# Row maxima of attention scores: small transfers in place of diagonal blocks, products with ones and row copies

## The chip, the cores and the metric

One core of a Trainium2 chip runs the kernel in one launch. The metric is the device time of one launch in microseconds (us); lower is better. The engines are PE (TensorE: matrix products), DVE (VectorE), ACT (ScalarE), POOL (GpSimd) and SP, which here only issues transfers (DMAs). Each engine works through its own list of instructions in order; semaphores hold an instruction back until what it needs is there.

## The reference

Two layers of a decoder trunk, 528 tokens (16 learned meta tokens and 512 real ones), width 1024. Each layer is a mixer (attention with 8 heads of 64, a 31-tap convolution group, a short gated convolution group, all from one input projection) and a gated feed-forward part with a 3-tap convolution. What matters here is the attention:

```python
F = jnp.cumsum(log_f, axis=1).transpose(0, 2, 1)
def attend(start, end):
    qb = q[:, start:end]
    s = jnp.einsum("bqhd,bkhd->bhqk", qb, k[:, :end]) * scale
    s = s + F[:, :, start:end, None] - F[:, :, None, :end]
    s = jnp.where(mask, s, NEG_INF)
    p = jax.nn.softmax(s, axis=-1)
    return jnp.einsum("bhqk,bkhd->bqhd", p, v[:, :end])
outs = [attend(0, N_META)]
for i in range((L - N_META) // Q_BLOCK):     # four blocks of 128 queries
    ...
```

The softmax needs for each query the maximum of its row of scores, so that the exponentials stay in range.

## The kernel before

Activations lie transposed: features on the 128 partitions, 528 tokens along the free dimension. Float32 accuracy comes from splitting each operand into a high and a low part, so that one product of the mathematics is three matrix products (`mm3`, L837; the value projection has its own loop, L1407). Most of the run is such products of a 128x128 block of weights with 264 tokens.

Each head has two query tiles and two key tiles (`qh[hd % 4]`, `kh[hd % 4]`, 128 partitions x 528). Half of the first pair's partitions hold the head's 64 features (high parts); some of the other partitions hold extra rows, among them the forget-gate sums on the key side. One extra row, `mrow` (`rows(hd)[2]`), is all ones in the key tile and, in the query tile, first zero and later minus the maximum of the query's row of scores. So the product of the two tiles gives scores less their maximum without a further instruction.

The mixer's work is written as threads: Python generators that yield what they wait for. A planner (`Flow`) steps them by a cost per instruction and thereby fixes the order of the instructions on each engine; on the chip this order is fixed and only the semaphores decide the times. Four threads matter. `maxima` and `exponentials` go head by head; `att_norms` normalises finished pairs of heads; `fill` makes the projections (blocks of 48 products, and 120 for the values) and so keeps PE at work while attention waits.

`maxima` before, for one head: five blocks of queries (`QB`: 16, then four of 128). For each block PE multiplies queries with keys (L1593; the last block takes two products), DVE takes the maximum of each row, with the causal mask added, into a column of `mcol` (L1600), one query to a partition. The maxima then have to come from a column into a row. POOL multiplies the identity with the column and with -1 into a block of the diagonal tile `dm` (L1608); PE multiplies `dm` with a matrix of ones, in two halves of 264 tokens, so that every row of the result holds all 528 negative maxima (L1617); ACT copies one row of it into `mrow` of the query tile (L1619). `maxima` of a head starts when `exponentials` of the head before has begun.

`exponentials` for one head: six blocks; per block PE makes the scores in two products (`logits`, L1637, the first reads `mrow`), ACT takes the exponential (L1644), POOL clears what lies above the diagonal (L1651), and two blocks later PE multiplies with the values (`weigh`, L1671; the trace records two instructions for each).

Transfers on SP in the mixer: weight blocks (`raw<-in_w_dram`, L785), gate rows (`k<-sq` and `k<-g_dram`, L699, from `gate_rows`), and for heads 2 to 7 the split projections of a pair of heads, from `pair_hi` and `pair_lo` into the query and key tiles (`part` and `spread`, L1499). The planner costs a gate row at `ROW_US` = 0.95 us of SP and the pair transfers at `PART_US` = 0.6 us and 2.2 us to landing. The query and key products of head 2 wait for the first `k<-pair_hi` of its pair. PSUM has two banks (`s1`) that `maxima`, the products with ones and the attention norms share.

Of the kernel before, what the change touches and what calls it, by code (L numbers as in the profile page):

```python
# [10 lines left out]
F32 = mybir.dt.float32  # L11
F32R = mybir.dt.float32r
BF16 = mybir.dt.bfloat16
AF = mybir.ActivationFunctionType
ALU = mybir.AluOpType

P = 128
D = 1024
KD = D // P
L = 528  # L20
N_META = 16
H = L // 2
# [40 lines left out]
PART_US, ROW_US = 0.6, 0.95  # L63
# [293 lines left out]
def mm_us(n, k=P):  # L357

    return max(n / 2400 + 0.012, 0.00086 * k)
# [7 lines left out]
def act_us(n):  # L367
    return 0.17 + 0.0009 * n
# [21 lines left out]
def tile_hybrid_trunk(ctx: ExitStack, tc: tile.TileContext, xT, wflat, pv_d, out):  # L390
    nc = tc.nc
# [3 lines left out]
    def T(pool, shape, dt, tag, bufs=None):  # L395
        uid[0] += 1
        kw = {} if bufs is None else {"bufs": bufs}
        return pool.tile(list(shape), dt, tag=tag, name=f"{tag}_{uid[0]}", **kw)
# [46 lines left out]
    ident = T(const, [P, P], F32, "ident")  # L445
    make_identity(nc, ident)
    def mset(t, val):
        nc.gpsimd.memset(t.bitcast(F32), val)
# [33 lines left out]
    flow = Flow()  # L482
# [5 lines left out]
    def half_sl(hf):  # L488
        return slice(H * hf, H * (hf + 1))
# [199 lines left out]
    def act(us, fn, *after, **kw):  # L689
        return flow.op("act", us, fn, after, **kw)  # L690
# [4 lines left out]
    def gp(us, fn, *after, **kw):  # L695
        return flow.op("pool", us, fn, after, **kw)
# [428 lines left out]
    def mixer(l, ypool, first, close_first, spans, front, rzs, u_at):  # L1125
# [125 lines left out]
        def bank(kind):  # L1251

            slot = yield from flow.grab(banks[kind])
            return psum[:, slot.buf], slot
# [104 lines left out]
        def rows(hd):  # L1359

            main = DH * (hd % 2)
            aux = DH - main
            return slice(main, main + DH), slice(aux, aux + DH), slice(aux + 32, aux + 33)

        for i in range(4):
# [3 lines left out]
            mset(kh[i][0][mrow], 1.0)  # L1369
            mset(qh[i][0][aux:aux + 32], 1.0)  # L1370
            mset(qh[i][0][aux + 32:aux + 64], 0.0)
        dms = []
        for j in range(2):
            dm = T(ap, [P, L], F32R, f"dm{j}")
            mset(dm[:, :N_META], 0.0)
            dms.append(dm)
        g_hl = [T(mp, [P, L], F32, "sq", 2)[:HEADS].bitcast(F32R) for _ in range(2)]

        v_at = {}
# [196 lines left out]

        def maxima():

            dm_at = {}
            for hd in range(HEADS):  # L1580
                yield [When(lambda: k_at.get(hd)), When(lambda: q_at[hd] if hd // 2 in k2_at else None),
                       When(lambda: gate_at.get(hd))] + ([When(lambda: begun.get(hd - 1))] if hd else [])
                q1, k1 = qh[hd % 4][0], kh[hd % 4][0]
                dm = dms[hd % 2]
                mcol = T(mp, [P, 6], F32, "mcol", 2)
                diag = []
                for b, (qs, n) in enumerate(QB):
                    end = qs + n
                    pieces = [(0, end)] if end <= 512 else [(0, H), (H, end)]
                    for i, (a, z) in enumerate(pieces):  # L1590
                        s, slot = yield from bank("s1")
                        s = s[:n, :z - a]
                        nc.tensor.matmul(s, lhsT=q1[:, qs:end], rhs=k1[:, a:z], start=True, stop=True)  # L1593
                        tok = flow.mm(mm_us(z - a, n))
                        last = z == end

                        def reduce(s=s, n=n, a=a, z=z, last=last, i=i, b=b):
                            junk = T(mp, [P, 400], BF16, "junk")
                            c0 = 400 - P + n - (z - a) if last else 0
                            nc.vector.tensor_tensor_reduce(  # L1600
                                junk[:n, :z - a], in0=s, in1=causal[:n, c0:c0 + z - a], scale=1.0,
                                scalar=-3e38 if i == 0 else mcol[:n, 5:6], op0=ALU.add, op1=ALU.max,
                                accum_out=mcol[:n, b:b + 1] if last else mcol[:n, 5:6])

                        d = dve(dve_us(z - a) + 0.08, reduce, tok, prio=0)
                        slot.close(d)
                        yield
                    diag.append(gp(0.5, lambda qs=qs, end=end, n=n, b=b: nc.gpsimd.tensor_scalar(  # L1608
                        dm[:n, qs:end], in0=ident[:n, :n], scalar1=mcol[:n, b:b + 1],
                        scalar2=-1.0, op0=ALU.mult, op1=ALU.mult), d, *dm_at.get(hd - 2, [zero])))  # L1610
                yield diag
                mrow = rows(hd)[2]
                toks, at = [], []
                for hf in range(2):
                    ps, slot = yield from bank("s1")
                    c = half_sl(hf)
                    nc.tensor.matmul(ps[:, :H], lhsT=ones_r, rhs=dm[:, c], start=True, stop=True)  # L1617
                    toks.append(flow.mm(mm_us(H)))
                    at.append(act(act_us(H), lambda ps=ps, c=c: nc.scalar.copy(q1[mrow, c], ps[mrow, :H]), toks[-1], prio=0))  # L1619
                    slot.close(at[-1])  # L1620
                    yield
                dm_at[hd] = toks
                max_at[hd] = at

        begun = {}
# [865 lines left out]
```

## Time and profile before

| | us |
|---|---|
| median of 3 runs (lowest, highest) | 1263.05 (1262.51, 1263.3) |
| span of the profiled execution, first to last instruction | 1262.4 |
| PE busy | 1243.7 (99%) |
| DVE, ACT, POOL busy | 926.1, 710.3, 174.6 |
| maxima and exponentials of layer 0 lie at about | 79 to 210 |
| and of layer 1 at about | 706 to 840 |

The profile gives no total for its execution beside the span; the span is 0.65 us under the median of the runs, and what is told of the span is applied to the median. Matrix products are pipelined, so that a busy PE can still lose time between products: a product of 264 tokens is recorded as about 0.28 us long, while the next one starts 0.12 us after it. The chain of work that ended last counts such products at their spacing.

### The profile page before, as it was taken

How to read it: one execution, taken by the hardware profiler on the slowest of the kernel's cores; microseconds unless marked ns; L12 is line 12 of the kernel's file. 1: busy time of each engine (PE TensorE's matmuls, PEld its weight loads, DVE VectorE, ACT ScalarE, POOL GpSimd, SP SyncE). 2: the span in 40 equal slices, each digit the busy share in tenths (PEclk: the TensorE clock that was granted, in tenths of full speed). 3: DMA queues.
4: the chain of work that ended last, by engine and by line, in shares of the span. 5: the costliest groups of instructions: out<-in, count | busy, mean ns of one | idle time of the engine just before them, and what ended most of it. 6: DMA issues, size and time to landing. Idle time of an engine off the chain costs nothing.

```text
span 1262.4 us, 24292 instructions
## 1 busy us (share of the span) xinstructions
PE 1243.7 (99%) x9554; PEld 1194.0 (95%) x9554; DVE 926.1 (73%) x1581; ACT 710.3 (56%) x1377; POOL 174.6 (14%) x360
## 2 busy tenths in 40 slices
PE   8999999999999999999999999999999999999997
PEld 8998898999999999999999988999999899989997
DVE  7887866589874776487688878656799748756964
ACT  7254576655444663476673545775554447526763
POOL 1323411001111001010003244120021000000000
PEclk9999999999999999999999999999999999999999
DMA  7357551726648755776652584547166565465611
GB/s 245 82 155 173 126 119 44 259 87 149 186 147 334 244 193 149 240 195 169 208 189 67 156 194 110 144 111 241 71 163 176 146 218 170 153 223 182 203 60 67
DMA packets 80755, 206.59 MB, mean 164 GB/s; under 512 B 8624, under 2 KB 18992, under 8 KB 80128
## 3 DMA queue, kind: packets, MB, share of 16 engines
q1 hardware_dynamic: 66976, 168.20, 42.1%
q0 software_dynamic: 13664, 36.84, 13.0%
q8 instruction: 75, 1.23, 0.4%
q14 instruction: 40, 0.33, 0.1%
HBM read 170.82 MB, written 50.60 MB: 175 GB/s over the span
## 4 chain that ended last, share of the span: by engine, by line
PE 89%; DVE 3%; issue 3%; DMA 2%; ACT 2%; POOL 1%; SPq 0%; DVEq 0%; POOLq 0%; ACTq 0%
PE psum L837 58%; PE psum L2288 17%; PE psum L1407 5%; PE psum L1671 3%; PE psum L1637 2%; PE psum L974 1%; PE psum L1593 1%; DMA raw<-in_w_dram 1%; PE psum L1737 1%; PE psum L1323 1%; DMA w_split<-slo 0%; DMA h<-in_w_dram 0%; POOL dm L1608 0%; DVE yp L1050 0%; DMA h<-in_x_dram 0%
## 5 line engine op out<-in xcount | busy, mean ns | idle before, releaser
L837 PE MATMUL psum<-y,whi 128*128 128x264 f32 (+3 forms) x1968 | 383.8, 299 | 0.8 <-DVE zs L989 0.7
L837 PEld LDWEIGHTS psum<-y,whi 128*128 128x128 f32 x1968 | 305.6, 188 | 13.8 <-DVE zs L989 0.9
L837 PE MATMUL psum<-uhi,whi 128*128 128x264 f32 (+1 forms) x1168 | 292.1, 289 | 1.5 <-ACT uhi L2069 0.7
L837 PE MATMUL psum<-ulo,whi 128*128 128x264 f32 (+1 forms) x1168 | 285.7, 284 | 0.6 <-DVE ulo L2071 0.4
L837 PE MATMUL psum<-uhi,wlo 128*128 128x264 f32 (+1 forms) x1168 | 285.1, 283 | 0.0
L837 PE MATMUL psum<-y,wlo 128*128 128x264 f32 (+3 forms) x984 | 273.7, 297 | 0.3 <-DVE wlo L793 0.3
L837 PEld LDWEIGHTS psum<-uhi,whi 128*128 128x128 f32 x1168 | 201.5, 188 | 6.2 <-issue 1.6
L837 PEld LDWEIGHTS psum<-ulo,whi 128*128 128x128 f32 x1168 | 201.6, 188 | 1.3 <-DVE ulo L2071 0.6
L837 PEld LDWEIGHTS psum<-uhi,wlo 128*128 128x128 f32 x1168 | 201.3, 188 | 0.0
L837 PEld LDWEIGHTS psum<-y,wlo 128*128 128x128 f32 x984 | 177.8, 188 | 5.8 <-DVE wlo L793 0.6
L2173 DVE SCALAR_TENSOR_TENSOR c<-zs,pv,c 128x528 f32<-128x528 f32 (+1 forms) x176 | 130.6, 756 | 23.5 <-ACT c L2171 22.2
L652 ACT CAST whi<-raw 128x1024 fp32r<-128x1024 f32 (+1 forms) x65 | 66.1, 1020 | 97.1 <-PE psum L837 74.5
L793 DVE TENSOR_TENSOR wlo<-raw,whi 128x1024 fp32r<-128x1024 f32 (+2 forms) x80 | 95.6, 1203 | 29.7 <-ACT whi L789 29.2
L789 ACT CAST whi<-raw 128x1024 fp32r<-128x1024 f32 (+2 forms) x80 | 81.7, 1031 | 24.9 <-PE psum L837 18.0
L653 DVE TENSOR_TENSOR wlo<-raw,whi 128x1024 fp32r<-128x1024 f32 (+1 forms) x65 | 76.9, 1183 | 21.1 <-ACT whi L652 21.0
L1153 DVE SCALAR_TENSOR_TENSOR cacc<-apad,pv,cacc 128x528 f32<-128x528 f32 x120 | 87.6, 772 | 0.1
L2288 PE MATMUL psum<-uhi,whi 128*128 128x258 f32 (+1 forms) x252 | 71.3, 284 | 0.0
L2288 PE MATMUL psum<-ulo,whi 128*128 128x258 f32 (+1 forms) x252 | 71.2, 283 | 0.0
L2288 PE MATMUL psum<-uhi,wlo 128*128 128x258 f32 (+1 forms) x252 | 70.7, 283 | 0.0
L2171 ACT ACTIVATE c<-zs,pv 128x528 f32<-128x528 f32 (+1 forms) x88 | 63.0, 727 | 6.8 <-DVE zs L2136 2.7
L2206 POOL COPY cols<-y 128x1 f32<-128x1 f32 x24 | 17.2, 716 | 335.8 <-ACT y L2187 335.5
L2288 PE MATMUL psum<-t,shi 128*128 128x258 f32 (+1 forms) x336 | 63.2, 283 | 0.0
(273 smaller groups left out, 2323.9 us busy)
## 6 DMA issues: line engine op xcount, KB each, us to landing
raw<-in_w_dram SPq DMA_DIRECT2D x114, 512.0 KB, 4.5
raw<-in_w_dram SPq DMA_DIRECT2D x30, 448.0 KB, 5.1
h<-in_w_dram SPq DMA_DIRECT2D x25, 512.0 KB, 4.5
raw<-w_sum SPq DMA_DIRECT2D x21, 512.0 KB, 5.4
h<-w_sum SPq DMA_DIRECT2D x21, 512.0 KB, 4.8
h<-in_w_dram POOLq DMA_DIRECT2D x16, 512.0 KB, 4.6
w_sum<-h POOLq DMA_DIRECT2D x16, 512.0 KB, 6.4
w_sum<-in_w_dram SPq DMA_DIRECT2D x26, 256.0 KB, 5.2
```

Source lines behind the costliest of these rows:

```text
L652: nc.scalar.copy(hi[:, :sz], raw[:, :sz])
L653: last_low[0] = nc.vector.tensor_sub(lo[:, :sz], raw[:, :sz], hi[:, :sz].bitcast(F32))
L789: nc.scalar.copy(box["hi"][:, :sz], box["raw"][:, :sz])
L793: nc.vector.tensor_sub(lo[:, :sz], box["raw"][:, :sz], box["hi"][:, :sz].bitcast(F32))
L837: nc.tensor.matmul(d, lhsT=w[a][:, k, cols], rhs=rhs(b, k, hf), start=start and i == 0 and p == 0, stop=stop and i == n - 1 and p == 2)
L1153: nc.vector.scalar_tensor_tensor(conv[j], in0=src, in1=conv[j], scalar=col("a_dw_w", CK * j + i), op0=ALU.mult, op1=ALU.add)
L1407: nc.tensor.matmul(ps[:n, :nw], lhsT=(uhi, ulo)[ui][:, k, P * b:P * b + n], rhs=w[wi][:, k % 4, :], start=k == 0 and p == 0, stop=k == KD ...
L1637: nc.tensor.matmul(s, lhsT=k[:, ka:ka + kn], rhs=q[:, s0:qz], start=i == 0, stop=i == 1)
L1671: nc.tensor.matmul(acc[:, s0 - qa:qz - qa], lhsT=vals[:, b].rearrange("p h d -> p (h d)")[:, o:o + P], rhs=box["p"], start=b == 0, stop=b ...
L2171: nc.scalar.activation(dst, src[:, 2:2 + 2 * fw], AF.Copy, scale=wtap(2, t))
L2173: nc.vector.scalar_tensor_tensor(dst, in0=src[:, i:i + 2 * fw], scalar=wtap(i, t), in1=dst, op0=ALU.mult, op1=ALU.add)
L2288: nc.tensor.matmul(psum[:, bank, :n7], lhsT=w[a][:, k0 + k, :], rhs=rhs(b, k), start=start and k == 0 and p == 0, stop=stop and k == K2 - ...
```

## The change

For each head, the diagonal blocks, the two products with ones and the two row copies go. In their place POOL negates the columns of maxima into a small tile `neg` in three instructions (after blocks 0, 2 and 4), and SP issues five transfers, one for each block of queries, that bring a column of `neg` (one element on each of up to 128 partitions) into the block's part of the row `mrow` of the query tile (up to 128 elements on one partition). The planner costs each at 0.95 us of SP and 3.5 us to landing, and makes a new order with them. The two tiles `dm` and their memsets go too. `neg` is doubled between heads as `mcol` is.

```diff
-        dms = []
-        for j in range(2):
-            dm = T(ap, [P, L], F32R, f"dm{j}")
-            mset(dm[:, :N_META], 0.0)
-            dms.append(dm)
...
-                dm = dms[hd % 2]
                 mcol = T(mp, [P, 6], F32, "mcol", 2)
-                diag = []
+                neg = T(mp, [P, 5], F32R, "neg", 2)
+                at = []
                 for b, (qs, n) in enumerate(QB):
...
-                    diag.append(gp(0.5, lambda qs=qs, end=end, n=n, b=b: nc.gpsimd.tensor_scalar(
-                        dm[:n, qs:end], in0=ident[:n, :n], scalar1=mcol[:n, b:b + 1],
-                        scalar2=-1.0, op0=ALU.mult, op1=ALU.mult), d, *dm_at.get(hd - 2, [zero])))
-                yield diag
-                mrow = rows(hd)[2]
-                toks, at = [], []
-                for hf in range(2):
-                    ps, slot = yield from bank("s1")
-                    c = half_sl(hf)
-                    nc.tensor.matmul(ps[:, :H], lhsT=ones_r, rhs=dm[:, c], start=True, stop=True)
-                    toks.append(flow.mm(mm_us(H)))
-                    at.append(act(act_us(H), lambda ps=ps, c=c: nc.scalar.copy(q1[mrow, c], ps[mrow, :H]), toks[-1], prio=0))
-                    slot.close(at[-1])
-                    yield
-                dm_at[hd] = toks
+                    if b in (0, 2, 4):
+                        mrow = rows(hd)[2]
+                        b0 = max(b - 1, 0)
+                        c = gp(0.2, lambda n=n, b0=b0, b=b: nc.gpsimd.tensor_scalar(
+                            neg[:n, b0:b + 1], in0=mcol[:n, b0:b + 1], scalar1=-1.0, scalar2=None, op0=ALU.mult), d)
+                        for i in range(b0, b + 1):
+                            qa, m = QB[i]
+                            at.append(flow.op("sp", ROW_US, lambda i=i, qa=qa, m=m: nc.sync.dma_start(
+                                q1[mrow, qa:qa + m].bitcast(F32), neg[:m, i:i + 1].bitcast(F32)), (c,), lat=3.5))
                 max_at[hd] = at
```

The new order is another one all through both mixers. Two places carry the prediction. The first is SP at the start of layer 0's attention. Before, the gate rows of heads 1 to 3 (`k_84`, `k_86`, `k_88`) are followed by two weight blocks and the copies for a sum of weights:

```order
L699 DMA k_84_698<-sq_733 1x16x33
L699 DMA k_86_700<-sq_732 1x16x33
L699 DMA k_86_700<-sq_733 1x16x33
L699 DMA k_88_702<-sq_732 1x16x33
L699 DMA k_88_702<-sq_733 1x16x33
L785 DMA raw_1155<-in_w_dram 128x1024
L785 DMA raw_1180<-in_w_dram 128x1024
L545 DMA w_sum_12_104_736<-in_w_dram 128x512 x2
```

Now the same stretch of SP holds head 0's five transfers (`q_90`) among the gate rows, and head 1's five (`q_92`) behind the copies (the changed kernel's L1609 is the new transfer):

```order
L1609 DMA q_90_704<-neg_1074 1x16x1
L699 DMA k_88_702<-sq_728 1x16x33
L1609 DMA q_90_704<-neg_1074 1x128x1 x2
L699 DMA k_88_702<-sq_729 1x16x33
L1609 DMA q_90_704<-neg_1074 1x128x1 x2
L785 DMA raw_1203<-in_w_dram 128x1024
L785 DMA raw_1217<-in_w_dram 128x1024
L545 DMA w_sum_12_102_732<-in_w_dram 128x512 x2
L545 DMA w_sum_12_102_732<-in_w_dram 128x1024
L1609 DMA q_92_706<-neg_1228 1x16x1
L1609 DMA q_92_706<-neg_1228 1x128x1 x4
```

The two weight blocks now stand behind head 0's last transfer, which waits for head 0's last maxima.

The second place is PE ahead of head 2's maxima (key tile `k_86`, query tile `q_94`). Before, PE is in the block of weights `whi_1147`, the one after the keys' block of this pair of heads, and 30 of its products stand between the last product of the keys' block and the first row of L1593 below:

```order
L837 MATMUL psum_67<-uhi_108,whi_1147 128x264
L837 MATMUL psum_67<-ulo_109,whi_1147 128x264
L837 MATMUL psum_67<-uhi_108,wlo_1162 128x264
L1593 MATMUL psum_67<-k_86_700,q_94_708 16x16
L1593 MATMUL psum_67<-k_86_700,q_94_708 128x144
```

Now the last product of the keys' block (`whi_1058`) is followed by nine rows of head 1's exponentials (L1625 is the scores, L1659 the product with the values, in the changed kernel's numbers), and then by head 2's maxima (L1587):

```order
L837 MATMUL psum_67<-uhi_108,wlo_1080 128x264
L1625 MATMUL psum_67<-q_92_706,k_84_698 128x128
L1625 MATMUL psum_67<-q_93_707,k_85_699 128x128
L1659 MATMUL psum_67<-p_79_687,vals_681 128x16
L1625 MATMUL psum_67<-q_92_706,k_84_698 128x400
L1625 MATMUL psum_67<-q_93_707,k_85_699 128x400
L1659 MATMUL psum_67<-pf_1381,vals_681 128x128
L1625 MATMUL psum_67<-q_92_706,k_84_698 128x400
L1625 MATMUL psum_67<-q_93_707,k_85_699 128x400
L1659 MATMUL psum_67<-pf_1392,vals_681 128x400
L1587 MATMUL psum_67<-k_86_700,q_94_708 16x16
L1587 MATMUL psum_67<-k_86_700,q_94_708 128x144
```

The 30 products moved behind head 2's first maxima. Layer 1 has the same two places in the same order.

More of the change, by code (lines that the diff above doesn't have):

```diff
@@ L1577, in maxima @@
         def maxima():
-            dm_at = {}
             for hd in range(HEADS):
```

## Prediction

> **What bounds the kernel now.** I read the busy shares first, then the two mixers in windows, then the instructions that go, then PE's waits, then the chain at the places that the new order changes. The page's first part and the two windows of the mixers (busy us of each engine with their counts, granted clock, DMA share, GB/s):
>
> ```profile
> PE 1243.7 (99%) x9554; PEld 1194.0 (95%) x9554; DVE 926.1 (73%) x1581; ACT 710.3 (56%) x1377; POOL 174.6 (14%) x360
> 76.80:213.50 136.70, 134.34 (x984) 122.32 (x984) 101.26 (x247) 85.86 (x224) 42.06 (x92) 1.00 0.50 124
> 706.00:840.50 134.50, 131.66 (x965) 120.14 (x964) 101.38 (x245) 83.55 (x220) 45.47 (x95) 1.00 0.58 139
> ```
>
> PE is the bound, in the mixers too: it is idle for 2.4 us of 136.7 and 2.8 us of 134.5, at full clock. ACT, DVE and POOL have a quarter of the time or more to spare, and the transfers take half of the DMA engines. So what leaves ACT and POOL is worth nothing by itself; what leaves PE counts, and so does each wait that comes or goes on PE.
>
> The instructions that go (count, then min/median/max in ns, first and last start), and PE's largest waits:
>
> ```profile
> L1608 POOL TENSOR_SCALAR dm<-ident,mcol x80: 267/372/1980, 80.9 to 819.8; 128x128 fp32r<-128x128 f32 x64, 16x16 fp32r<-16x16 f32 x16
> L1617 PE MATMUL psum<-dm,ones_r x32: 279/288/485, 84.3 to 829.9; 128*128 128x264 f32 x32
> L1619 ACT CAST q<-psum x32: 364/370/374, 84.8 to 830.2; 1x264 fp32r<-1x264 f32 x32
> PE psum L1617 <- POOL dm L1608: 1.4, 2, 1.0
> PE psum L1593 <- issue: 1.2, 1, 1.2
> PE psum L1593 <- DMA k<-pair_hi: 1.1, 1, 1.1
> PE psum L1323 <- ACT q L1619: 0.8, 2, 0.4
> ```
>
> Two of these four waits belong to what goes: PE waits for the diagonal, and a norm's product (L1323) waits for the bank that the row copy still holds. The other two are one wait, seen in each layer: head 2's maxima wait for the keys of their pair.
>
> **The change part by part.** *Products with ones.* In the chain, products are told at their spacing:
>
> ```profile
> 84.18 0.45 PE psum L1323 x2
> 84.63 0.25 PE psum L1617 x2
> 101.42 7.62 PE psum L837 x63
> ```
>
> Two products with ones take 0.25 us, the same 0.12 each as L837 (7.62/63 = 0.121). The record of 0.288 us is the length in the pipe, not the price. 32 of them are 32 x 0.121 = 3.9 us of PE. Gain: 3.9 us. A bound from above is 32 x 0.288 = 9.2, but that counts overlapped time, so I leave it out of the range.
>
> *Waits that go.* 1.4 us (diagonal) and 0.8 us (row copy), both PE's own. Gain: 2.2 us; from below nothing, if the same bank or DVE holds PE up elsewhere.
>
> *ACT, POOL, DVE.* ACT loses 32 x 0.37 = 11.8 us, POOL 80 diagonal blocks, and gets 48 small negations. Nothing shows one of this shape; the nearest rows are a memset of 128x16 (below) and the diagonal block's 0.372. I take 0.3 us, near the second, since both read and write a column; the range of 0.12 to 0.37 matters only in the latency below. DVE's list keeps its 96 maxima. All of this is beside PE: 0 us. The cover is PE's products, and if it were gone POOL's part would be worth what the waits above show.
>
> *SP.* 80 more issues, on a queue that is mostly idle, held by its buffers (258.2 us in the row below for one pair of lines alone). Rows: the memset; the gate rows' issues in layer 1 (one row of 528 numbers each) and their landing; the landing of all pair transfers; SP's longest wait.
>
> ```profile
> L448 POOL MEMSET dm<- x4: 116/117/118, 57.4 to 688.1; 128x16 f32 x4
> L699 SPq DMA_DIRECT2D k<-sq x8: 497/542/585, 702.3 to 708.9; - x8
> DMA to landing us min/median/max: 2.0/2.0/2.0
> DMA to landing us min/median/max: 2.3/3.8/5.3
> SPq L785 <- DVE wlo L793: 258.2, 51, 25.1
> ```
>
> An issue costs 0.54 us, so 80 cost 43 us of SP over 271 us of mixers. Behind a transfer that waits for maxima stand others: at the first place shown above, two weight blocks. They leave SP at 81.85 now (first row below); then they leave when head 0's last two transfers have: the last diagonal block starts at 83.92, plus 0.37 and two issues of 0.54, about 85.4. That is 3.5 us later. The cast that first needs one of them comes at 97.66, and a block of 512 KB lands 4.5 us after its issue (page, last part), at about 90. So this costs 0, and the cover is 7 us deep.
>
> ```profile
> 81.85 4.52 SPq L785 DMA_DIRECT2D raw<-in_w_dram  x2
> 82.81 0.28 PE L1593 MATMUL psum<-k,q 128*128 128x264 f32 x1
> 83.92 0.37 POOL L1608 TENSOR_SCALAR dm<-ident,mcol 128x128 fp32r<-128x128 f32 x1 [0.86 <-DVE mcol L1600]
> 97.66 1.04 ACT L789 CAST whi<-raw 128x1024 fp32r<-128x1024 f32 x1
> raw<-in_w_dram SPq DMA_DIRECT2D x114, 512.0 KB, 4.5
> ```
>
> *The new latency.* The scores of a head (L1637) now wait for the last transfer. From the last product of the maxima to the maxima in place is 83.92 - 82.81 = 1.1 us; then the negation 0.3, the first of its two issues 0.54, and the second's landing. No row shows a transfer of 128 single elements. The nearest rows are the gate rows: from one partition to one, little data, landing in 2.0 us. The pair transfers, with 60 times a gate row's bytes, bound it from above with 5.3. I take 2.0 to 2.5 and get 1.1 + 0.3 + 0.54 + 2.3 = 4.2 us. What covers it is the work that the new order puts on PE between a head's last product of maxima and its first scores. For head 0 that is 39 products and two norm products, 39 x 0.121 + 2 x 0.45 = 5.6 us; for heads 1 to 7 it is 51, 57, 27, 57, 48, 48 and 24 products, where the two small counts have four or five blocks of exponentials (about 1 us each) beside them: 6 to 8 us. So almost all is hidden. I put 0.5 us for the lot.
>
> The Trainium skill's page "DMA: Bandwidth & Descriptors" speaks against the change here: its section "Rules for kernel authors" says to coalesce small transfers, since under 64 KB one pays mostly overhead, and that a last dimension that is not contiguous becomes one descriptor per element; "Anatomy of one DMA" puts the fixed part at about 2.0 us. The gate rows agree with the 2.0, but they also show that eight such transfers, issued 0.54 apart, each land in 2.0, so that the overheads overlap and only the last one's is seen. By five fixed parts in a row, an estimate from that page of 10 us a head, the covers above would be too short by some 4 us for each of 16 heads and the kernel some 60 us slower; by the rows the sum stays as it is.
>
> *Head 2's keys.* The one place where the new order costs. The chain in both layers, before, ahead of head 2's maxima, and the same blocks of scores and weighing for head 1 (in order: scores 128, weighing 16, scores 400, weighing 128, scores 400, weighing 400):
>
> ```profile
> 109.04 1.20 issue
> 733.07 0.40 ACT pair_hi L1542
> 733.49 4.05 DMA k<-pair_hi
> 737.54 0.25 issue
> 737.79 0.34 PE psum L1593 x2
> ...
> 93.72 0.17 PE psum L1637 x2
> 94.31 0.13 PE psum L1671 x2
> 94.44 0.46 PE psum L1637 x2
> 96.37 0.22 PE psum L1671 x2
> 96.59 0.37 PE psum L1637 x2
> 97.69 0.67 PE psum L1671 x2
> ```
>
> From ACT's copy of the last keys at 733.07 to the maxima at 737.79 are 4.7 us, 4.05 of them the transfer. Before, 30 products (30 x 0.121 = 3.6 us) stand between the last keys' product and the maxima, and PE waits 1.2 and 1.1 us. In the new order they stand behind the maxima, and the nine rows in their place take 0.17 + 0.13 + 0.46 + 0.22 + 0.37 + 0.67 = 2.0 us. The wait therefore grows by 3.6 - 2.0 = 1.6 us in each layer. Loss: 3.2 us. Bounds: from below 0, if the keys land 1.6 us sooner (2.3, the shortest landing above, would do it); from above 2 x 2.8, if the landing is at 5.3. What hid the transfer is late next: the 30 products themselves, which delay nobody, since PE has them anyway.
>
> *Sum.* -3.9 - 2.2 + 0.5 + 3.2 = -2.4 us against the span of 1262.4. The span lies 0.65 under the median, so I apply it there: 1263.05 - 2.4 = 1260.65. Since PE is the bound after the mixers as well, I assume that the rest of the run is only shifted. A new order throughout two mixers usually brings small waits of its own; the 2.4 and 2.8 us of idle PE above are what this one has, so I round to 1261.0.
>
> **The rivals.** *The keys come in time (gain of 6).* If head 2's transfers land in 2.3 us, the shortest row, the wait at head 2 does not grow: -3.9 - 2.2 + 0.5 = -5.6, 1257.4; with the old wait gone too, 1255.2. For it: the pair transfers' median is 3.8. Against it: 4.05 and about the same at 105.9 to 110.2 in layer 0, with the same transfers ahead of them in the new order.
>
> *The small transfers are late (slower).* The mechanism is at each head's first scores on PE: a transfer of 128 elements of 4 bytes lands later than a row, or sits behind weight blocks in the same queue. At a landing of 5.3 the latency is 1.1 + 0.37 + 0.54 + 5.3 = 7.3 us: 1.7 too late for head 0 and about 0.5 for the others, 2 x (1.7 + 7 x 0.5) = 10 us, less the 0.5 already in: 1261 + 9.5 = 1270.5. It decides the sign at a mean landing of about 4.6, where only head 0 and the short covers are late by 1 us (2.4 us in all). For it: the median of the pair transfers is 3.8 at a DMA share of 0.5 to 0.6. Against: those carry 132 KB, mostly queued behind each other.
>
> A rule of the same page bears on this one: "Specifications" there says that a transfer below 512 B makes the engine read, modify and write. No run here shows what that adds; the gate rows, in pieces of 132 B, land in 2.0 with it.
>
> *Nothing moves.* PE's 3.9 us come back as waits for weights or for DVE, which still does 101 us of 137: 1263. Against it: PE's idle time before is under 2%.
>
> **How the numbers follow.** A difference of 0.2%, 2.5 us, is about what this measurement tells from none. Chances: the forecast (hidden transfers, longer wait at head 2) 0.50, between 1259 and 1263.5, with the line of 1260.5 in it, so 0.20 faster, 0.28 same and 0.02 slower; the keys in time 0.20, all faster; late transfers 0.20, all slower; nothing moves 0.10, same. Together faster 0.40, same 0.38, slower 0.22. The range: down to 1256.5, which takes in most of the second case, and up to 1267, which takes in the milder half of the third; about 1 in 10 is left out at the top and less below. The forecast's own range is 1259 to 1263.5.
>
> **What the profile of the changed kernel would show.** The row of PE's waits for L1617 and that of L1323 on ACT's row copy are gone; PE's count falls by 32. The wait of head 2's maxima for `k<-pair_hi` stands at 2.5 to 3 us in each layer: at 1.2 or less the second case holds. The new transfers land in 2.0 to 2.5 us, with an issue of about 0.5; if that is 4 or more, and L1637 (now L1625) waits for `q<-neg` in the chain, the third holds. I am wrong in another way if PE waits for weights (`wlo`) or for the maxima's banks in the mixers, or if time is lost outside them.

## The result and the profile after

| | median us | lowest, highest | runs |
|---|---|---|---|
| before | 1262.94 | 1262.51, 1263.30 | 4 |
| after | 1270.92 | 1269.81, 1272.61 | 4 |

The changed kernel takes 1.0064 times as long [1.0050, 1.0079]: 8.0 us slower, above the range of the prediction. The profiled execution of the changed kernel is its fastest (1269.81), with a span of 1268.1 us, 5.7 us longer than the span of before. The other three ran at a mean granted clock of 0.995 in place of 1.000; the last section comes to that. The spans differ by less than the medians because the profiled execution of before was a long one: in the 73 later executions of before whose span is recorded, the span is 1.65 to 1.8 us below the time, so that a span of 1262.4 belongs to some 1264.1 us, 1.2 above the median.

The page's first part, the mixers in windows, the transfers' packets and the new instructions, as read of before:

```profile
PE 1239.7 (98%) x9522; PEld 1188.9 (94%) x9522; DVE 926.7 (73%) x1581; ACT 699.2 (55%) x1345; POOL 154.5 (12%) x324
76.80:220.00 143.20, 134.93 (x981) 121.59 (x980) 102.66 (x252) 82.68 (x215) 32.98 (x80) 1.00 0.50 118
707.00:850.00 143.00, 135.63 (x988) 122.31 (x988) 105.12 (x254) 81.56 (x213) 35.49 (x79) 1.00 0.58 134
DMA packets 90482, 206.61 MB, mean 163 GB/s; under 512 B 18352, under 2 KB 28720, under 8 KB 89856
L1609 SPq DMA_DIRECT2D q<-neg x80: 468/550/1069, 81.3 to 831.2; - x80
L1605 POOL TENSOR_SCALAR neg<-mcol x48: 212/216/695, 81.0 to 830.3; 128x2 fp32r<-128x2 f32 x32, 16x1 fp32r<-16x1 f32 x16
```

The work went as announced: 32 products and 32 copies fewer, 80 transfers more, an issue in 0.55 us and a negation in 0.22. But PE, idle for 2.4 and 2.8 us of the mixers before, is now idle for 143.2 - 134.9 = 8.3 and 143.0 - 135.6 = 7.4 us. PE's waits name the places (line, what it waited for, us in total, times, longest):

```profile
PE psum L1587 <- DVE mcol L1594: 5.3, 2, 3.1
PE psum L1659 <- POOL pf L1639: 4.2, 2, 2.1
PE psum L837 <- DVE pair_lo L1540: 4.1, 4, 1.1
PE psum L1323 <- DVE cxp L1215: 1.2, 2, 0.6
PE psum L837 <- DVE wlo L793: 1.0, 2, 0.6
```

Of the first three rows before had only the second, much smaller:

```profile
PE psum L1671 <- POOL pf L1651: 0.6, 2, 0.3
```

The scores (now L1625) never wait for `q<-neg`, and head 2's maxima (now L1587) do not wait for `k<-pair_hi`. The largest waits are ones that the prediction did not have: maxima that wait for DVE, and head 1's weighing (now L1659) that waits for POOL's clearing `pf`. Why PE waits for `pair_lo` (twice in each layer, at other places) was not followed up.

The first two have one stretch of layer 0 in common (layer 1 has the same). From the chain of work (start, us, what):

```profile
103.87 1.26 POOL pf L1639
...
107.33 7.80 DMA raw<-in_w_dram
115.13 0.02 issue
115.15 0.63 ACT pw L789
...
122.57 0.39 PE psum L1587
```

and from the timelines of POOL, DVE and PE there (in brackets the idle time before, and what ended it):

```profile
103.87 1.25 POOL L1639 TENSOR_SCALAR_AFFINE_SELECT pf<-pf 128x128 f32<-128x128 f32 x1 [5.54 <-ACT pf L1632]
105.07 1.23 POOL L534 DMA_DIRECT2D w_sum<-in_w_dram  x1
106.85 0.34 POOL L1639 TENSOR_SCALAR_AFFINE_SELECT pf<-pf 128x128 f32<-128x128 f32 x1 [0.55 <-ACT pf L1632]
103.75 1.22 DVE L793 TENSOR_TENSOR wlo<-raw,whi 128x1024 fp32r<-128x1024 f32 x1
115.80 0.69 DVE L793 TENSOR_TENSOR pw<-raw,pw 128x512 fp32r<-128x512 f32 x1 [4.77 <-ACT pw L789]
122.57 0.39 PE L1587 MATMUL psum<-k,q 128*128 128x272 f32 x1 [3.08 <-DVE mcol L1594]
```

Read from the top: the new order puts head 1's scores 63 products later, directly ahead of their weighing, with none of `fill`'s products between, so that PE has nothing to do while ACT takes the exponential and POOL clears a block (2.1 us; the clearing itself takes 1.25 us here, with a subtraction of DVE beside it, in place of the usual 0.29). Behind that clearing POOL issues a weight-sum transfer. `pw`, a block of weights on SP, is issued 2.3 us after it, right behind the transfers of a pair, and takes 7.8 us to land; ACT, in order, stands at its cast, DVE stands behind ACT for 4.8 us, DVE then has a queue to work off, and head 3's maxima wait for it for 3.1 us.

### The profile page after: what moved, and what is told of

Same layout as the page of the kernel before. It is cut to its first block, busy times and chain, and to the rows that moved or that the text cites. A ratio compares the mean times of both kernels' runs of the same rounds, so it can differ in the third digit from the quotient of the medians.

```text
span 1268.1 us, 24363 instructions
## 1 busy us (share of the span) xinstructions
PE 1239.7 (98%) x9522; PEld 1188.9 (94%) x9522; DVE 926.7 (73%) x1581; ACT 699.2 (55%) x1345; POOL 154.5 (12%) x324
## 4 chain that ended last, share of the span: by engine, by line
PE 90%; DVE 4%; DMA 2%; ACT 2%; issue 1%; POOL 0%; SPq 0%; DVEq 0%; POOLq 0%; ACTq 0%
PE psum L837 61%; PE psum L2276 17%; PE psum L1402 5%; PE psum L1659 3%; DMA raw<-in_w_dram 2%; PE psum L974 2%; PE psum L1625 1%; DVE cacc L1153 1%; DVE wlo L793 1%; PE psum L1587 1%; PE psum L1725 1%; PE psum L1323 0%; DVE junk L1594 0%; DMA h<-in_x_dram 0%; PE psum L1777 0%
## 5 line engine op out<-in xcount | busy, mean ns | idle before, releaser
L2194 POOL COPY cols<-y 128x1 f32<-128x1 f32 x24 | 16.4, 685 | 337.4 <-ACT y L2175 337.2
```

## The experiments

All are timed beside the kernel before on the same chip, whose median was 1262.5 to 1263.5 in them. Theory 1: the loss is in the new order and in what it brings together. Theory 2: it is in the transfers, by SP's time or by their landing.

**The transfers left out, in the changed kernel's own order.** The edit, beside the constant in the row:

```diff
-  at.append(flow.op("sp", ROW_US, lambda i=i, qa=qa, m=m: nc.sync.dma_start(...), (c,), lat=3.5))
+  at.append(flow.op("sp", ROW_US, lambda: None, (c,), lat=3.5))
```

> The changed kernel in its own order of instructions on PE, ACT and DVE, but the 80 small transfers are not issued, and the row that they would fill holds the constant -10 (left out: the use of the row maxima). Theory 1, the loss is in the new order that the planner makes of the transfers' assumed cost (0.95 us of SP each, 3.5 us to land), and in what that order brings together: about 1270, within 1.5 us of the changed kernel, with DVE mcol, POOL pf and DVE pair_lo still in PE's list of waits at 3 to 5 us each. Theory 2, the transfers themselves cost it, by SP's time or by their landing: 1257 to 1263, and those waits are mostly gone.

**The transfers made, into tiles that nobody reads.**

```diff
-  q1[mrow, qa:qa + m].bitcast(F32), neg[:m, i:i + 1].bitcast(F32))
+  aside[hd % 2][mrow, qa:qa + m].bitcast(F32), neg[:m, i:i + 1].bitcast(F32))
```

> The changed kernel with its 80 transfers issued as they are, but into two tiles that nobody reads, and the row of the maxima held at the constant -10 (left out: the use of the row maxima). SP keeps its load, nobody waits for a landing. Theory 1 (the order): about 1270, as the changed kernel and as the version without transfers. Theory 2 by SP's time (weight blocks behind small transfers): about 1270 too, while the version without transfers is at 1257 to 1263. Theory 2 by the landing: this one falls to 1257 to 1263.

Measured: 1270.00 without the transfers (1.0056 [1.0044, 1.0068]) and 1271.49 with them aside (1.0068 [1.0055, 1.0081]). Both are where the changed kernel is: each interval holds its 1.0064. In this order the 80 transfers, their time on SP and their landing cost nothing that the intervals tell from zero (the difference of 1 us is uncertain by about 2): theory 2 falls as the cause of the 8 us. One detail of the expectation missed. Without transfers PE's waits are

```profile
PE psum L1659 <- POOL pf L1639: 4.2, 2, 2.1
PE psum L837 <- DVE pair_lo L1541: 4.1, 4, 1.1
PE psum L1588 <- DVE mcol L1595: 1.1, 2, 0.9
```

with the wait for maxima 4.2 us shorter, and still the span is 1268.3. There the granted clock fell after the wait for `pf`, in each layer for a stretch of 3.4 us at half clock, worth up to 1.7 us. PE therefore reaches these maxima later, and the wait is shorter without the maxima being much earlier: from the weighing that waited for `pf` to the maxima that waited pass 17.4 us in the changed kernel (105.18 to 122.57) and 16.4 here (105.48 to 121.90). The small transfers do not make `pw` late either: here it is issued at 106.79 and cast at 114.53, 7.7 us later.

**`pw` loaded early.** One transfer per layer is moved to the mixer's start, into a tile of its own:

```diff
+  pw_raw[l] = T(ap, [P, 512], F32, "pw_raw")
+  nc.sync.dma_start(pw_raw[l], flat_w(...))      # at the mixer's start
...
+  if chunks[i][0] == "a_pw_w":
+      box["raw"] = pw_raw[chunks[i][1]]
+      return
```

> The changed kernel with one transfer per layer moved: the weight block pw of the mixer is loaded at the mixer's start into a tile of its own, everything else in its place in the order. Theory 1 in its closer form: ACT stands at the cast of pw, whose block lands late behind the weight-sum transfer, DVE stands behind ACT, and PE then waits for head 3's maxima (3.08 and 2.17 us). Then these two waits go and the time falls by 4 to 6 us, to about 1265. Rival: the maxima of head 3 are late for another reason (DVE has too much to do there by the new order): the same to within 1 us.

Measured: 1265.20 (1.0025 [1.0014, 1.0036]), 5.7 us below the changed kernel, as expected. (At a mean clock of 1.000 the two take 1263.8 to 1264.6 and 1269.8 us; at 0.994 to 0.997, 1267.7 to 1270.7 and 1270.6 to 1272.6.) The row of `mcol` is gone from PE's waits; these two stay as they were:

```profile
PE psum L1665 <- POOL pf L1645: 4.2, 2, 2.1
PE psum L841 <- DVE pair_lo L1546: 4.1, 4, 1.1
```

So `pw`'s late block is some two thirds of the loss by the medians, and it has nothing to do with maxima except that the new order moved it. Why it takes 7.8 us was not tried apart. In layer 0 of before it is issued at 110.55, after that weight-sum transfer has landed, and ACT does not wait for it; in layer 1 it is issued at 737.75, ACT waits 0.17 us, and the cast starts at 742.32. That speaks for the weight-sum transfer in flight, but the pair transfers ahead of it on SP are a rival.

**What the removed work is worth.** The kernel before in its own order, with the matrix products with ones, the copies and the diagonal blocks planned but not issued:

```diff
-  nc.tensor.matmul(ps[:, :H], lhsT=ones_r, rhs=dm[:, c], start=True, stop=True)
-  lambda ps=ps, c=c: nc.scalar.copy(q1[mrow, c], ps[mrow, :H])
+  lambda: None
```

> The kernel before in its own order, with the diagonal blocks, the 32 products with ones and the row copies planned but not issued, and the row of the maxima at the constant -10 (left out: the use of the row maxima). It measures the first two terms of the prediction's sum by themselves. By the prediction: 3.9 + 2.2 = 6.1 us faster than before, about 1256.6. Rival: PE's 3.9 us come back as waits for DVE or for weights, 1259 to 1263.

Measured: 1259.19 (0.9967 [0.9955, 0.9980]), 3.5 us faster. That is about the 3.9 us of the products alone. The two waits went, and two of the same size came: at the maxima, which now come earlier, for a gate row (`k<-sq`), and at the norms' products (L1323), for DVE. The other two rows, at head 2's maxima, before had as well:

```profile
PE psum L1323 <- DVE cxp L1215: 1.3, 2, 0.6
PE psum L1594 <- issue: 1.4, 1, 1.4
PE psum L1594 <- DMA k<-sq: 1.2, 1, 1.2
PE psum L1594 <- DMA k<-pair_hi: 0.9, 1, 0.9
```

This is about what the change can bring in the old order if the transfers are hidden at no cost.

**The change in the old order.** Each diagonal block becomes a negation and a transfer at its old place:

```diff
+  nc.gpsimd.tensor_scalar(neg[:n, b:b + 1], in0=mcol[:n, b:b + 1], scalar1=-1.0, scalar2=None, op0=ALU.mult)
+  nc.sync.dma_start(q1[mrow, qs:end].bitcast(F32), neg[:n, b:b + 1].bitcast(F32))
```

> The change in the order of the kernel before: each diagonal block becomes a negated column and a small transfer issued at the same place, products with ones and row copies are not issued. Scores follow the maxima as closely as before (18, 9, 24, 30, 9, 75, 12 and 54 products between them). If the transfers take the 4 us that the prediction put and their wait falls on PE wherever fewer than some 30 products stand between: five heads of eight, 1 to 2 us each, in two layers, so 1256.6 + 10 to 18 = 1267 to 1275, with q<-neg as the largest of PE's waits. If the old order had cover enough: 1257 to 1260, and the planner's move of the scores was needless.

Measured: 1277.18 (1.0107 [1.0092, 1.0123]), 2 us above the expected range, with the wait at the scores that the second rival described, and a landing of 4.5 us for head 0's last transfer (the first row is from PE's waits, the second from the chain). The range had no term for the clock, which in the trace stands at half for three stretches of 6.8 us behind these waits, worth up to 10 us:

```profile
PE psum L1639 <- DMA q<-neg: 12.8, 6, 4.4
85.63 4.53 DMA q<-neg
```

So the landing is not short, and the planner was right to move the scores away: its order, though slower than before, is some 6 us faster than this one.

**The same on POOL's queue.** POOL issues the transfer itself, behind the negation:

```diff
-  nc.sync.dma_start(q1[mrow, qs:end].bitcast(F32), neg[:n, b:b + 1].bitcast(F32))
+  nc.gpsimd.dma_start(q1[mrow, qs:end].bitcast(F32), neg[:n, b:b + 1].bitcast(F32))
```

> The change in the old order as in the experiment before (1277.2), with one thing altered: the small transfers are issued by POOL, right behind the negation, on POOL's queue, in place of SP's. If a small transfer is late because its 4-byte packets stand behind SP's weight blocks and pair transfers on the same queue, the wait for q<-neg falls from 12.8 us to under 6, few or no dips of the clock are left, and the time is 1262 to 1268. If it is late because the DMA engines are shared whichever queue it is on, or if POOL's issue takes longer, it stays at 1272 to 1280.

Measured: 1294.97 (1.0251 [1.0237, 1.0266]): outside both expectations, with a mean granted clock of 0.988. On POOL's queue the trace gives the landing of all 80, and the wait is no smaller; POOL's issues (0.59 us each) also stand ahead of the clearing:

```profile
DMA to landing us min/median/max: 1.5/2.3/6.3
PE psum L1639 <- DMA q<-neg: 13.6, 8, 4.4
PE psum L1673 <- POOL pf L1653: 7.7, 9, 1.6
```

The queue is not what makes some of them late. On SP's queue few traces tell landings; that of the version planned at 3.5 us with `pw` early (below) tells 14 of 80, with the same spread:

```profile
DMA to landing us min/median/max: 1.7/3.3/7.1
```

**Other planned costs.** Here only numbers in the planner change, so that it makes other orders of the same work. The first has the transfers at what an undisturbed one takes:

```diff
-  at.append(flow.op("sp", ROW_US, ..., lat=3.5))
+  at.append(flow.op("sp", 0.55, ..., lat=2.2))
```

> The changed kernel with the transfers planned at what they were measured to take (0.55 us of SP, 2.2 us to land) in place of 0.95 and 3.5; the planner then makes another order, in which head 1's scores stand earlier. Theory 1: the new order brings back the products between scores and weighing, the wait for POOL pf goes, and the time is 1260 to 1266. Theory 2 (the transfers themselves): 1268 to 1273. If any new order brings waits of this size by chance, it is anywhere between, with its waits at other places.

Measured: 1269.27 (1.0054 [1.0041, 1.0066]), the third case. The waits for `pf` and most of that for `mcol` are gone; 4.0 us for `q<-neg` and 1.4 for `k<-pair_hi` are there instead. With `pw` early, and 2.8 or 3.5 us to land:

> The changed kernel with the weight block pw loaded early into its own tile, as in the experiment above, and the transfers planned at 0.55 us of SP and 2.8 us to land. Head 1's scores then stand at product 330 in place of 360, and head 2's maxima at 390, as before the change. Theory 1: neither the waits for POOL pf (2 x 2.1) nor those for head 3's maxima are left, PE never idles as much as 2 us, the clock stays at full, and the time is 1257 to 1261, below the kernel before. If small transfers land at 4 us where pair transfers stand ahead of them on the queue, PE waits for q<-neg for 2 to 4 us and it is 1261 to 1265.

> As the last, with 0.55 us of SP and 3.5 us to land: head 1's scores at product 342, head 2's maxima at 384. More cover for the landing, less for head 1's weighing. Theory 1: 1257 to 1262, no wait for q<-neg, perhaps 1 us per layer for POOL pf. If the order is what counts and each new one brings its own waits, it differs from the last by 2 us or more to either side.

Measured: 1264.26 (1.0012 [1.0003, 1.0021]) and 1266.42 (1.0025 [1.0016, 1.0034]). The first shows what was possible. Where the next stage's products `uhi,whi` begin and end (of before, of before without the work, and of this kernel):

```profile
L2288 PE MATMUL psum<-uhi,whi x252: 277/284/293, 435.5 to 1191.3; 128*128 128x258 f32 x72, 128*128 128x264 f32 x54
L2286 PE MATMUL psum<-uhi,whi x252: 277/284/293, 432.6 to 1186.0; 128*128 128x258 f32 x72, 128*128 128x264 f32 x54
L2282 PE MATMUL psum<-uhi,whi x252: 277/284/293, 431.9 to 1191.3; 128*128 128x258 f32 x72, 128*128 128x264 f32 x54
```

After layer 0 it is 3.6 us ahead of before, more than the version without the work (2.9). In layer 1 it loses them again, the largest part where two small transfers follow a weight block and pair transfers (SP's timeline, and the chain):

```profile
734.20 0.53 SPq L789 DMA_DIRECT2D raw<-in_w_dram  x1
735.17 1.15 SPq L1615 DMA_DIRECT2D q<-neg  x2
736.42 1.83 SPq L1500 DMA_DIRECT2D q<-pair_hi  x3
735.77 6.44 DMA q<-neg
742.28 4.42 DMA q<-neg
```

One lands after 6.4 us; another is issued only then and takes 4.4; PE waits 2.2 us for it, and the clock is at half for 3.4 us behind that wait. The waits for `pf` are gone, as theory 1 had it, and the time is in the range for late transfers. The second kernel of the pair shows no wait over 1.1 us in its mixers and runs at full clock, and yet takes 1264 to 1268; what spreads its runs stayed open. With the transfers on POOL's queue in such orders:

> The changed kernel with the weight block pw loaded early and the transfers on POOL's queue, planned at 0.55 us of POOL and 2.8 us to land; head 1's scores stand at product 330. If the queue is what made them late: no wait for q<-neg over 1 us, full clock, 1258 to 1261, the first version below the kernel before. If the engines are: a wait of 2 to 4 us as on SP's queue (1264.3), 1262 to 1266.

> The same with 3.5 us to land: head 1's scores at product 342. More cover: if the last still shows a wait for q<-neg, this one does not, and it is the faster of the two, at 1258 to 1262; if the order makes new waits for DVE or POOL, as the like one on SP's queue (1266.4), 1262 to 1267.

Measured: 1269.76 (1.0061 [1.0044, 1.0077]) and 1271.88 (1.0063 [1.0050, 1.0077]); the wait for `q<-neg` is 4.6 and 6.2 us, so neither beats SP's queue, and both times are above either expected range.

**The clearing planned longer.** With `pw` early, three orders:

```diff
-  a = gp(0.33, clear, a, prio=0)
+  a = gp(0.8, clear, a, prio=0)
```

> The changed kernel with pw loaded early and POOL's clearing of the exponentials' upper triangle (pf) planned at 0.8 us in place of 0.33; transfers planned as in the changed kernel (0.95 and 3.5). If pf's wait (4.2 us) is what is left: PE's wait for POOL pf falls under 1 us and the time to 1260 to 1262. If any new order brings waits of its own: the wait goes, others of 2 to 5 us come, 1263 to 1267.

> The same with the transfers planned at 0.55 us of SP and 4.2 us to land: head 1's scores at product 348, with more cover for the landing than the orders of 330 and 342. First theory: neither pf nor q<-neg is waited for over 1 us, 1259 to 1261. Second: 1262 to 1267.

> The same with 0.75 us of SP and 3.5 us to land, an order that differs from the last in a few dozen places. First theory: 1259 to 1262, within 1 us of the last. Second: the three orders differ from each other by 2 us or more, without a cause that the planned costs would name.

Measured: 1281.55 (1.0150 [1.0137, 1.0164]), 1273.52 (1.0086 [1.0072, 1.0100]) and 1271.04 (1.0065 [1.0051, 1.0079]). The wait for `pf` shrinks or goes, and a wait for the keys of head 2 comes up. The first order:

```profile
PE psum L1631 <- DMA k<-pair_hi: 6.0, 1, 6.0
PE psum L1593 <- DMA k<-pair_hi: 4.8, 1, 4.8
PE psum L1665 <- POOL pf L1645: 2.3, 4, 0.7
```

The first theory is wrong in all three, and the second, that other waits come, is too mild: its ranges ended at 1267. This is the wait for head 2's keys that the prediction had. It put 2.5 to 3 us in each layer; the three orders show 6.0 and 4.8, 4.8 and 2.9, 3.4 and 2.6 (the 6.0 at head 1's scores, just ahead of the maxima).

**The pair transfers planned at the landing that they have**, 4.5 us in place of 2.2, with `pw` early; and the kernel before with that edit alone, as a control:

```diff
-  after, lat=2.2)
+  after, lat=4.5)
```

> The changed kernel with pw loaded early, the small transfers planned at 0.55 us of SP and 2.8 us to land, and the pair transfers at 4.5 us to land in place of 2.2. If the planned landings were the cause: no wait of PE over 2 us in the mixers, full clock, 1257 to 1261. If orders bring their own waits: 1263 to 1270.

> The same with 4.2 us to land for the small transfers. First theory: 1257 to 1261, no wait for q<-neg, since the longest landing on SP's queue beside blocks was 6.4 and most are under 3. Second: 1263 to 1270, with pf waited for, as in the other orders in which head 1's scores stand past product 350.

> The kernel before with the pair transfers planned at 4.5 us to land and nothing else: the control. The wait for head 2's keys (1.2 and 1.1 us) goes. If a planned landing near the measured one is worth it by itself: 1260 to 1262. If a new order is a draw: anywhere from 1260 to 1268.

Measured: 1264.14 (1.0007 [0.9998, 1.0016]), 1270.43 (1.0059 [1.0045, 1.0073]), and the control 1267.61 (1.0039 [1.0027, 1.0052]). The first is the best version with transfers, level with before. The control says most: the same instructions as before, the wait for head 2's keys gone, and yet 4 to 5 us slower, at full clock. Small waits stand at other places, of which before had the last alone, with 0.3 us:

```profile
PE psum L837 <- DVE pair_lo L1545: 2.1, 2, 1.0
PE psum L1671 <- ACT yta L1685: 1.2, 2, 1.0
PE psum L837 <- DVE rs_t L1292: 1.2, 2, 0.9
PE psum L837 <- DVE wlo L793: 0.9, 2, 0.6
```

They are not the whole loss. In the mixers' windows of before (76.8 to 213.5 and 706 to 840.5) PE is idle for 6.2 us in place of 5.2; the page gives PE 1245.3 us of busy time in place of 1243.7 for the same 9554 products. Where that time goes between the products was not found.

No version beat the kernel before; only the one that leaves the work out is faster.

## Why the prediction was wrong, point by point

*Products with ones, 3.9 us gained:* right as far as it shows: with the waits, whose gain did not come, 3.5 measured (2.5 to 5.7 by the interval).

*Waits that go, 2.2 us:* wrong. The diagonal's and the row copy's waits went, but waits of the same size came at the maxima and at the norms' products (1.3 us for DVE there without the work, 1.2 in the changed kernel, in place of 0.8). The prediction named this case ("nothing from below") and then booked the whole amount.

*The latency of the transfers, 0.5 us:* right in its result, in the changed kernel's order nobody waits for them. The size behind it was wrong: not 2.0 to 2.5 us but 1.5 to 7.9 where the traces on POOL's queue tell it, up to 6.4 in the chains shown of SP's, and 4.5 at head 0's place in the old order. Its rows were also thinner than it took them to be: the trace of before tells the landing of one of the eight gate rows in the fence (2.0 us) and of 12 of the 72 pair transfers, so that all eight land in 2.0 was not read from it. The rule of the Trainium skill's page "DMA: Bandwidth & Descriptors" ("Rules for kernel authors"), by which the prediction put some 60 us against it, does not show either: 80 transfers of single elements, left out altogether, save 1 us, which the intervals don't tell from nothing. (The fixed part of 2.0 us that the estimate of 60 us rests on is given on that page of the Trainium skill, in "Anatomy of one DMA", for transfers that POOL issues; these are SP's.) They are hidden because the planner, with its 0.95 and 3.5, moved the scores far away. That move has a price, and the sum has no term for it but the 0.35 us of rounding.

*SP's order, 0 us:* the step that failed most. It looked at one place, the two weight blocks at layer 0's start, found 7 us of cover, and went on. Another weight block, `pw`, 20 us later, stands behind pair transfers and beside a weight-sum transfer in the new order and lands after 7.8 us. Moving it alone gives back 5.7 us of the 8.0. The wait is not at a product that needs the weights but at maxima, by way of ACT and DVE: the sign that the prediction gave last (PE waiting for the maxima's banks), without its cause.

*ACT, DVE and POOL beside PE, 0 us:* wrong for the same reason. That these engines have a quarter of their time to spare over a mixer says nothing of a stretch in which each stands in order behind one late block.

*Head 2's keys, 3.2 us lost:* not in the changed kernel, where nothing waits for these keys. PE stands at `pf` ahead of these maxima, 2.1 us in each layer, and the keys land meanwhile: in layer 0 the first is issued at 103.20, and the maxima start at 106.77 without a wait; 2.1 us earlier they would have started 1.5 us after the issue, sooner than any pair transfer told in a trace of before lands (2.3). The wait is real in other orders: 6.0 to 10.8 us in the three with the clearing planned longer. Others without a wait of 2 us for `pf` at this place show 0 to 2.3. That the 4.2 us for `pf` are near the 3.2 of this term is chance.

*Late transfers, the rival at 1270.5:* near the measured time by accident. Its mechanism, PE at the scores for `q<-neg`, is not in the changed kernel; it is what happens in the old order (12.8 us).

The sum by the windows: PE's idle time in the mixers was 2.4 + 2.8 = 5.2 us and is 8.3 + 7.4 = 15.7 (the five rows of waits shown of after add up to 15.8). That is 10.5 more; less 3.9 for the products it is 6.6, and the span grew by 5.7. The median grew by 8.0: the profiled execution of before was 1.2 us above its median, and that of the changed kernel 1.1 below its own, the one run of four at full clock.

That a new order brings small waits of its own was said, and rounded to 0.35 us. The control shows 4 to 5 us for a reordering that adds and removes nothing, and the other planned orders of this work, with the transfers on SP, lie between 1264 and 1282. A range that ends at 1267 did not take that in.

## What to carry to other kernels

In a schedule that keeps the bound engine 98% busy, a change that makes a planner order everything anew has to be charged for the order: time one or two reorderings of the unchanged work first, and take their spread as the least uncertainty of any forecast. A transfer that is hidden is not free; ask what was moved to hide it, and follow each load that now meets another one to all engines that stand in order behind it, not only to the bound one. When a wait is taken away, look what it covered: here the wait for `pf` stood where the keys landed, and in the three orders that planned it away a longer wait for the keys came up.

## What the runs showed of the hardware

*A wait of 2 us on PE can cost another 1.7.* In the version without transfers, three windows of 3.41 us in a row, with their PE busy time and, third from the right, the granted clock:

```profile
102.40:105.81 3.41, 1.31 (x11) 0.98 (x10) 2.95 (x5) 2.66 (x6) 1.63 (x2) 1.00 0.88 230
105.81:109.22 3.41, 3.41 (x11) 2.06 (x10) 2.02 (x7) 1.04 (x3) 1.30 (x3) 0.50 0.77 159
109.22:112.64 3.42, 3.42 (x24) 2.93 (x24) 1.98 (x8) 0.86 (x3) 2.03 (x6) 1.00 1.02 220
```

After a window with 1.31 us of work the clock is halved for one window, worth 1.7 us of PE; in other traces it is halved for two in a row (6.83 us), once for three. Within a trace the changes of the clock lie a whole number of such windows apart, on a fixed grid. In the mixers of all the traces, each of the 29 windows with less than 1.75 us of work was followed by half clock; of those with 1.75 to 2.2 us four were (one of them itself at half clock) and 18 were not; above 2.2 us none at full clock was. By this, whether a wait is punished depends on where it falls in the grid, which stands elsewhere against the start of the span in each trace (the first change comes 4.1 to 6.9 us after it). That would explain why one kernel has two sorts of runs: the version with `pw` early took 1263.8 to 1264.6 us in runs at 1.000 and 1267.7 to 1270.7 in those at 0.994 to 0.997. Only one of its runs has a trace, so this is not shown. The Trainium skill's page "TensorE: Matmul & The Clock Gate" has the free-running window of 3413 ns ("What's actually happening"), and the rows agree; its advice to leave no gaps above about 3 us ("Why this matters for your kernels") sets the limit too high for this case, where a single gap of 2.1 us was followed by half clock.

*POOL's clearing takes up to four times as long beside one of DVE's subtractions.* Of 80 clearings in the changed kernel's mixers 15 overlap the making of a low weight part on DVE (`wlo`, two operands from memory) and take 0.44 to 1.26 us, 0.82 in the middle; the other 65 have a median of 0.29 (the longest two, 1.3, stand beside other instructions of DVE). The first in the fence of POOL's and DVE's timelines above is one of the 15. The Trainium skill's page "GPSIMD Engine Reference", section "Specifications", says that the two engines share their memory interfaces and that an instruction of DVE with two such operands contends; the rows fit it, and no run here tried it apart.

*Small transfers take 1.5 us to land or 6, on the same kernel.* The long ones stand among larger transfers. In the three versions on POOL's queue, where the traces tell all 240 landings, the 106 under 2.2 us had one weight block, weight sum or pair transfer on average issued in the 6 us before them or during them, the 54 over 4 us had eight. On SP's queue the two traces that tell some of them show up to 7.1 and 9.9 us.
